# Mixture-of-experts combine: rounds of nine tokens with one summed on TensorE, in place of rounds of ten on VectorE

## The chip, the cores and the metric

The kernel runs on one core of a Trainium2 chip. The metric is the device time of one execution in microseconds (us). The profile's span, from the first to the last instruction, is a little shorter than that time.

## The reference

```python
batch, seq, n_experts, expert_dim = 16, 1024, 8, 512

def reference(expert_outputs, combine_weights):
    weights = combine_weights[..., np.newaxis]
    return np.sum(expert_outputs * weights, axis=2).astype(np.float32)
```

There are 16 x 1024 = 16,384 tokens. Each has eight expert outputs of 512 fp32 numbers (16 KB) and eight weights. The output of a token is the weighted sum of its eight rows (2 KB). Every input number is used once, so 268 MB come in and 34 MB go out, with a multiply and an add for each input number.

## The kernel before

Tokens lie on 128 partitions, so each partition has 128 tokens. "A token" below means one token on each partition: 128 x 16 KB. The tile `ring` holds ten tokens (`R = 10`). A round loads them in three chunks of four, four and two; a group, one pass of VectorE's hardware loop, is two rounds. Twelve rounds take 120 tokens; a tail of eight follows.

```python
R = 10
G = 2 * R
M = 2 * G
T_P = T // P
GROUPS = T_P // G
LOOP = GROUPS * G
TAIL = T_P - LOOP
ROUNDS = LOOP // R
CHUNKS = [(0, 4), (4, 4), (8, 2)]
# ... (cut)
x_g = x[0:cut].rearrange("(n p b g) e d -> n b p g e d", p=P, b=2, g=G)
# ... (cut)
pe_e = [6, 6, 6, 6, 5, 5, 5, 4]
tail_stores = [(0, 4), (4, 2), (6, 1), (7, 1)]
```

In the loop VectorE does all the arithmetic. For a chunk it makes one product with the first expert's weight, over all the chunk's tokens, and then for each token seven fused multiply-adds, each over 512 numbers. `take` waits on a semaphore and takes the amount off it again.

```python
with nc.Fori(0, GROUPS, engines=OrderedEngineSet([vector.engine])):
    for h in range(2):
        take(w_set[h], 1)
        for c, (r, m) in enumerate(CHUNKS):
            take(loaded[c], 16)
            q = h * R + r
            i = vector.tensor_tensor(
                out=acc[:, q : q + m],
                in0=ring[:, r : r + m, 0],
                in1=w_c[:, q : q + m, 0:1].to_broadcast([P, m, D]),
                op=mult,
            )
            # ... (cut)
            for g in range(q, q + m, 2):
                for e in range(1, E):
                    for k in (g, g + 1):
                        i = fused(k, e, w_c[:, k, e : e + 1], acc[:, k])
                        # ... (cut: waits and counts)
    take(step, last["all"])
```

SyncE issues the loads. A chunk is loaded again as soon as VectorE has finished its tokens of the round before. Once the loop's loads are out, the eight tail tokens are loaded one by one as slots come free, then the last round and the tail are stored.

```python
def loads_and_last_stores(sync):
    for n in range(ROUNDS):
        for c, (r, m) in enumerate(CHUNKS):
            if n:
                sync.wait_ge(done, (n - 1) * R + r + m)
            # ... (cut: the load of chunk c of round n; the weights after the first)
    for j in range(TAIL):
        sync.wait_ge(done, LOOP - R + j + 1)
        sync.dma_start(out=ring[:, j], in_=x_t[:, j]).then_inc(tail_in[j], 16)
    store(sync, ROUNDS - 1)
    for j, m in tail_stores:
        sync.wait_ge(done, LOOP + j + m)
        sync.dma_start(out=o_t[:, j : j + m], in_=acc[:, j : j + m]).then_inc(tail_out, 16)
```

ScalarE copies each round's weights to `w_c`, issues the stores of the other rounds, and in the tail multiplies the identity matrix by single weights, which gives diagonal matrices. TensorE multiplies them with the first four to six experts' rows of the tail tokens and sums in PSUM; VectorE does the other experts of the tail.

```python
def first_terms(tensor):
    for k, (j, e) in enumerate(diags):
        if e == 0:
            tensor.wait_ge(tail_in[j], 16)
        tensor.wait_ge(diag_set, k + 1)
        tensor.matmul(ps[:, j], lhsT=diag[:, k % DIAGS], rhs=ring[:, j, e],
                      start=e == 0, stop=e == pe_e[j] - 1).then_inc(product, 1)
```

Of the kernel before, what the change touches and what calls it, by code (L numbers as in the profile page):

```python
# [10 lines left out]
def kernel(  # L11
# [17 lines left out]

    nc = tc.nc  # L30
    fp32 = mybir.dt.float32
    mult, add = mybir.AluOpType.mult, mybir.AluOpType.add

    B, S, E, D = expert_outputs.shape
    T = B * S
    P = 128
    R = 10
    G = 2 * R
    M = 2 * G
    T_P = T // P  # L40
    GROUPS = T_P // G
    LOOP = GROUPS * G
    TAIL = T_P - LOOP
    ROUNDS = LOOP // R
    CHUNKS = [(0, 4), (4, 4), (8, 2)]
    C = len(CHUNKS)
    DIAGS = 5
# [3 lines left out]
    o = out.rearrange("b s d -> (b s) d")  # L51
    cut = LOOP * P
    x_g = x[0:cut].rearrange("(n p b g) e d -> n b p g e d", p=P, b=2, g=G)
    w_g = w[0:cut].rearrange("(n p m) e -> p n m e", p=P, m=M)
    o_g = o[0:cut].rearrange("(n p b g) d -> n b p g d", p=P, b=2, g=G)
    x_t = x[cut:T].rearrange("(p j) e d -> p j e d", j=TAIL)
    w_x = w[cut:T].rearrange("(p j) e -> p j e", j=TAIL)
    o_t = o[cut:T].rearrange("(p j) d -> p j d", j=TAIL)


    pe_e = [6, 6, 6, 6, 5, 5, 5, 4]
    tail_stores = [(0, 4), (4, 2), (6, 1), (7, 1)]
    diags = [(j, e) for j in range(TAIL) for e in range(pe_e[j])]
# [4 lines left out]
    acc = one.tile([P, G, D], fp32, name="acc")  # L68
    w_t = one.tile([P, T_P, E], fp32, name="w_t")
    w_c = one.tile([P, G, E], fp32, name="w_c")  # L70
    ident = one.tile([P, P], fp32, name="ident")
    diag = one.tile([P, DIAGS, P], fp32, name="diag")
    ps = psum.tile([P, TAIL, D], fp32, name="ps")
# [4 lines left out]
    loaded = [sem(f"loaded{c}") for c in range(C)]  # L78
    stored = [sem(f"stored{h}") for h in range(2)]
    step = sem("step")  # L80
    done = sem("done")
    tail_in = [sem(f"tail_in{j}") for j in range(TAIL)]
    tail_out = sem("tail_out")
    id_set = sem("id_set")
    diag_set = sem("diag_set")
    product = sem("product")

    def store(queue, n):
        h = n % 2
        queue.wait_ge(done, (n + 1) * R)  # L90
        queue.dma_start(
            out=o_g[n // 4, n // 2 % 2, :, h * R : h * R + R], in_=acc[:, h * R : h * R + R]
        ).then_inc(stored[h], 16)

    def loads_and_last_stores(sync):
        for n in range(ROUNDS):
            for c, (r, m) in enumerate(CHUNKS):
                if n:
                    sync.wait_ge(done, (n - 1) * R + r + m)
                g = n % 2 * R + r  # L100
                sync.dma_start(
                    out=ring[:, r : r + m], in_=x_g[n // 4, n // 2 % 2, :, g : g + m]
                ).then_inc(loaded[c], 16)
                if n == 0 and c == 0:
                    sync.dma_start(
                        out=w_t[:, 0:LOOP].rearrange("p (n m) e -> p n m e", m=M), in_=w_g
                    ).then_inc(w_in, 16)
                    sync.dma_start(out=w_t[:, LOOP:T_P], in_=w_x).then_inc(w_in, 16)
        for j in range(TAIL):
            sync.wait_ge(done, LOOP - R + j + 1)  # L110
            sync.dma_start(out=ring[:, j], in_=x_t[:, j]).then_inc(tail_in[j], 16)
        store(sync, ROUNDS - 1)
        for j, m in tail_stores:
            sync.wait_ge(done, LOOP + j + m)
            sync.dma_start(out=o_t[:, j : j + m], in_=acc[:, j : j + m]).then_inc(tail_out, 16)
# [13 lines left out]
    def weights_and_stores(scalar):  # L129
        scalar.wait_ge(w_in, 32)  # L130
        for n in range(ROUNDS):
            h = n % 2
            if n >= 2:
                store(scalar, n - 2)
                scalar.wait_ge(stored[h], 16 * (n // 2))
            scalar.copy(  # L136
                out=w_c[:, h * R : h * R + R], in_=w_t[:, n * R : n * R + R]
            ).then_inc(w_set[h], 1)
        store(scalar, ROUNDS - 2)
        scalar.wait_ge(stored[0], 16 * ROUNDS // 2)  # L140
        scalar.wait_ge(id_set, 2)
        for k, (j, e) in enumerate(diags):
            i = scalar.mul(out=diag[:, k % DIAGS], in_=ident, mul=w_t[:, LOOP + j, e : e + 1])  # L143
            i.then_inc(diag_set, 1)
            if k >= DIAGS:
                i.wait_op(product, k - DIAGS + 1, "sem-ge")
        scalar.wait_ge(stored[1], 16 * ROUNDS // 2)
        scalar.wait_ge(tail_out, 16 * len(tail_stores))

    def first_terms(tensor):  # L150
        for k, (j, e) in enumerate(diags):
            if e == 0:
                tensor.wait_ge(tail_in[j], 16)
            tensor.wait_ge(diag_set, k + 1)
            tensor.matmul(  # L155
                ps[:, j],
                lhsT=diag[:, k % DIAGS],
                rhs=ring[:, j, e],
                start=e == 0,
                stop=e == pe_e[j] - 1,  # L160
            ).then_inc(product, 1)

    def terms(vector):
        def take(s, v):
            vector.wait_ge(s, v).then_inc(s, -v)  # L165

        last = {}

        def count(i, g, e):

            if e == E - 1:
                i.then_inc(done, 1)
            else:
                i.then_inc(step, 1)
                last["all"] = last.get("all", 0) + 1
                last[g] = last["all"]

        def fused(g, e, weight, before):
            return vector.scalar_tensor_tensor(  # L179
                out=acc[:, g], in0=ring[:, g % R, e], scalar=weight, in1=before, op0=mult, op1=add  # L180
            )

        with nc.Fori(0, GROUPS, engines=OrderedEngineSet([vector.engine])):
            for h in range(2):
                take(w_set[h], 1)
                for c, (r, m) in enumerate(CHUNKS):
                    take(loaded[c], 16)
                    q = h * R + r
                    i = vector.tensor_tensor(  # L189
                        out=acc[:, q : q + m],  # L190
                        in0=ring[:, r : r + m, 0],
                        in1=w_c[:, q : q + m, 0:1].to_broadcast([P, m, D]),
                        op=mult,
                    )
                    i.then_inc(step, 1)
                    last["all"] = last.get("all", 0) + 1
                    last.update((g, last["all"]) for g in range(q, q + m))
                    for g in range(q, q + m, 2):
                        for e in range(1, E):
                            for k in (g, g + 1):  # L200
                                i = fused(k, e, w_c[:, k, e : e + 1], acc[:, k])
                                i.wait_op(step, last[k], "sem-ge")
                                count(i, k, e)
            take(step, last["all"])

        last.clear()
        for q in ((0, 1), (2,), (3,), (4,), (5,), (6,)):
            for e in range(pe_e[q[0]], E):
                for j in q:
                    weight = w_t[:, LOOP + j, e : e + 1]  # L210
                    if e == pe_e[j]:
                        i = fused(j, e, weight, ps[:, j])
                        i.wait_op(product, sum(pe_e[: j + 1]), "sem-ge")
                    else:
                        i = fused(j, e, weight, acc[:, j])
                        i.wait_op(step, last[j], "sem-ge")
                    count(i, j, e)

        j = TAIL - 1
        for e in range(pe_e[j], E):  # L220
            weight = w_t[:, LOOP + j, e : e + 1]
            if e == pe_e[j]:
                i = vector.tensor_scalar_mul(out=acc[:, j], in0=ring[:, j, e], scalar1=weight)  # L223
                i.wait_op(tail_in[j], 16, "sem-ge")
            else:
                i = fused(j, e, weight, acc[:, j])
                i.wait_op(step, last[j], "sem-ge")
            count(i, j, -1)
        vector.wait_ge(step, last[j])  # L229
        i = vector.tensor_tensor(out=acc[:, j], in0=acc[:, j], in1=ps[:, j], op=add)  # L230
        i.wait_op(product, len(diags), "sem-ge")
        count(i, j, E - 1)

    with tc.tile_critical(no_gpsimd_drain=True):  # L234
        loads_and_last_stores(nc.sync)
        identity(nc.gpsimd)
        weights_and_stores(nc.scalar)
        first_terms(nc.tensor)
        terms(nc.vector)
# [30 lines left out]
```

## Time and profile before

| | us |
|---|---|
| time, median of three | 707.33 (707.19 to 707.56) |
| span of the profiled execution | 705.5 |
| VectorE busy | 642.8 |
| TensorE busy, all of it in the tail | 38.7 |
| ScalarE busy | 21.1 |
| transfers in the span | 302.5 MB |

The profile's first part gives each engine's busy time and its share of the span. A second part cuts the span in 40 slices, with one digit of busy tenths for each, for the engines and for the 16 DMA engines together. The groups of instructions are listed by line, engine and operation, with the output and input tiles, their shapes, the count, the busy time, the mean length of one, and the idle time of that engine just before them with what ended it. Records of one engine may overlap, so that a mean can be longer than the pace at which instructions follow each other. DVE is VectorE, ACT ScalarE, PE TensorE, SP SyncE; a name with q is the engine's queue of waits and DMA issues.

### The profile page before, as it was taken

The page shows a single profiled execution, that of the slowest core. Times are in us where ns is not written, and L with a number is a line of the kernel's source. Part 1 is how long each engine was busy: PE and PEld are TensorE (multiplying, and loading weights), DVE is VectorE, ACT ScalarE, POOL GpSimd, SP SyncE. Part 2 cuts the span into 40 slices and gives each one's busy share as a digit, 9 for nine tenths or more (in the row PEclk, how much of TensorE's full clock was granted, in tenths as well). Part 3 has the DMA queues.
Part 4 walks back from the last instruction along what each step waited for, and adds up shares of the span by engine and source line. Part 5 has one row for each costly group of instructions (what it writes and reads, how often), then busy time and mean ns, then how long its engine had stood idle before and what let it go on. Part 6 is the DMA issues. An engine that isn't in the chain of part 4 may idle for free. (4 is left out here: it accounts for less than half of the span.)

```text
span 705.5 us, 1328 instructions
## 1 busy us (share of the span) xinstructions
PE 38.7 (5%) x86; PEld 16.9 (2%) x86; DVE 642.8 (91%) x898; ACT 21.1 (3%) x56; POOL 0.7 (0%) x6
## 2 busy tenths in 40 slices
PE   0000000000000000000000000000000000000695
PEld 0000000000000000000000000000000000000242
DVE  0599999979999989989999998998998998998964
ACT  0000000000000000000000000000000000000241
POOL 0000000000000000000000000000000000000000
PEclk9999999999999999999999999999999999999999
DMA  9999999999999999999999999999999999999997
GB/s 412 390 472 420 394 435 446 450 412 461 403 444 446 445 404 429 435 428 475 430 401 447 416 432 434 472 394 468 416 441 421 420 440 463 431 426 407 430 428 334
DMA packets 9186, 302.53 MB, mean 429 GB/s; under 512 B 1120, under 2 KB 1504, under 8 KB 1888
## 3 DMA queue, kind: packets, MB, share of 16 engines
q1 hardware_dynamic: 7600, 273.68, 90.0%
q10 hardware_dynamic: 1584, 28.84, 9.5%
q14 instruction: 2, 0.02, 0.0%
HBM read 268.96 MB, written 33.55 MB: 429 GB/s over the span
## 5 line engine op out<-in xcount | busy, mean ns | idle before, releaser
L179 DVE SCALAR_TENSOR_TENSOR acc<-ring,w_c,acc 128x512 f32<-128x512 f32 x840 | 559.7, 745 | 1.3
L189 DVE TENSOR_TENSOR acc<-ring,w_c 128x2048 f32<-128x2048 f32 (+1 forms) x36 | 69.5, 1931 | 46.2 <-DVEq L165 46.2
L155 PE MATMUL ps<-ring,diag 128*128 128x512 f32 x86 | 38.7, 613 | 659.1 <-DMA ring<-in_expert_outputs_dram 659.1
L155 PEld LDWEIGHTS ps<-ring,diag 128*128 128x128 f32 x86 | 16.9, 198 | 680.1 <-DMA ring<-in_expert_outputs_dram 659.1
L136 ACT COPY w_c<-w_t 128x80 f32<-128x80 f32 x12 | 3.0, 258 | 587.5 <-DMA out_dram<-acc 565.3
L143 ACT ACTIVATE diag<-ident,w_t 128x128 f32<-128x128 f32 x43 | 16.8, 400 | 84.4 <-DMA out_dram<-acc 54.2
L179 DVE SCALAR_TENSOR_TENSOR acc<-ring,w_t,ps 128x512 f32<-128x512 f32 x7 | 5.1, 744 | 9.6 <-PE ps L155 9.6
L179 DVE SCALAR_TENSOR_TENSOR acc<-ring,w_t,acc 128x512 f32<-128x512 f32 x13 | 9.7, 751 | 0.4
L136 ACT ACT_TABLE_LOAD x1 | 1.3, 1283 | 0.9 <-SPq L234 0.9
L230 DVE TENSOR_TENSOR acc<-acc,ps 128x512 f32<-128x512 f32 x1 | 0.7, 689 | 0.1
L223 DVE TENSOR_SCALAR acc<-ring,w_t 128x512 f32<-128x512 f32 x1 | 0.5, 481 | 0.0
L119 POOL TENSOR_SCALAR_AFFINE_SELECT ident<-ident 128x128 f32<-128x128 f32 x1 | 0.3, 292 | 0.1
L118 POOL MEMSET ident<- 128x128 f32 x1 | 0.2, 204 | 0.5 <-SPq L234 0.5
L254 POOL MEMSET const-bfloat16-1.0<- 128x1 bf16 x1 | 0.1, 101 | 0.0
L254 POOL MEMSET const-uint8-127<- 128x1 uint8 x1 | 0.1, 101 | 0.0
L254 POOL MEMSET const-float32-0.0<- 128x1 f32 x1 | 0.1, 98 | 0.2 <-issue 0.2
L254 POOL MEMSET const-float32-1.0<- 128x1 f32 x1 | 0.1, 98 | 0.0
## 6 DMA issues: line engine op xcount, KB each, us to landing
ring<-in_expert_outputs_dram SPq DMA_DIRECT2D x12, 4096.0 KB, 34.0
out_dram<-acc ACTq DMA_DIRECT2D x11, 2560.0 KB, 26.7
ring<-in_expert_outputs_dram SPq DMA_DIRECT2D x8, 2048.0 KB, 28.6
out_dram<-acc SPq DMA_DIRECT2D x1, 2560.0 KB, 24.8
out_dram<-acc SPq DMA_DIRECT2D x1, 1024.0 KB, 17.7
out_dram<-acc SPq DMA_DIRECT2D x1, 512.0 KB, 9.0
out_dram<-acc SPq DMA_DIRECT2D x2, 256.0 KB, 4.7
w_t<-in_combine_weights_dram SPq DMA_DIRECT2D x1, 480.0 KB, 22.6
```

The lines of the kernel that those rows point to most:

```text
L118: gpsimd.memset(ident, 0.0).then_inc(id_set, 1)
L119: gpsimd.affine_select(out=ident, in_=ident, compare_op=mybir.AluOpType.not_equal, fill=1.0, base=0, pattern=[[-1, P]], channel_multiplier ...
L136: scalar.copy(out=w_c[:, h * R : h * R + R], in_=w_t[:, n * R : n * R + R]).then_inc(w_set[h], 1)
L143: i = scalar.mul(out=diag[:, k % DIAGS], in_=ident, mul=w_t[:, LOOP + j, e : e + 1])
L155: tensor.matmul(ps[:, j], lhsT=diag[:, k % DIAGS], rhs=ring[:, j, e], start=e == 0, stop=e == pe_e[j] - 1,).then_inc(product, 1)
L179: return vector.scalar_tensor_tensor(out=acc[:, g], in0=ring[:, g % R, e], scalar=weight, in1=before, op0=mult, op1=add)
L189: i = vector.tensor_tensor(out=acc[:, q : q + m], in0=ring[:, r : r + m, 0], in1=w_c[:, q : q + m, 0:1].to_broadcast([P, m, D]), op=mult,)
L223: i = vector.tensor_scalar_mul(out=acc[:, j], in0=ring[:, j, e], scalar1=weight)
L230: i = vector.tensor_tensor(out=acc[:, j], in0=acc[:, j], in1=ps[:, j], op=add)
L254: nc = _bacc.Bacc("TRN2", target_bir_lowering=False, num_devices=1)
```

## The change

The ring holds nine tokens instead of ten, in three chunks of three. Fourteen rounds take 126 tokens and leave a tail of two. Per round VectorE sums eight tokens; the ninth, the last of the third chunk, goes to TensorE: VectorE makes all its eight diagonal matrices with one product, TensorE runs eight products in a loop of its own, and ScalarE copies the sum from PSUM to `acc`. This is meant to take work from VectorE, to leave little for the tail, and to have the slots come free in equal chunks. VectorE's loop is placed at a chosen instruction slot (`head_slot`), so that it begins in the second block of instructions. 126 tokens a partition are laid out as two blocks, 54 and 72 consecutive tokens on each partition, instead of three of 40. The stores of the last two rounds are held back until the tail's loads have been issued, and the tail is stored in one piece. In the tail TensorE does the first four experts and VectorE the last four.

The core of the diff:

```diff
-    R = 10
+    R = 9
+    C = 3
     G = 2 * R
-    M = 2 * G
+    BLOCKS = (6 * R, 8 * R)
# ... (cut: sizes and layouts)
+    HELD = 2
+    K = 4
# ...
     def loads_and_last_stores(sync):
         for n in range(ROUNDS):
-            for c, (r, m) in enumerate(CHUNKS):
+            for c in range(CHUNKS):
                 if n:
-                    sync.wait_ge(done, (n - 1) * R + r + m)
+                    sync.wait_ge(summed[c], n * C)
# ...
+        sync.wait_ge(summed[0], ROUNDS * C)
         for j in range(TAIL):
-            sync.wait_ge(done, LOOP - R + j + 1)
             sync.dma_start(out=ring[:, j], in_=x_t[:, j]).then_inc(tail_in[j], 16)
-        store(sync, ROUNDS - 1)
-        for j, m in tail_stores:
-            sync.wait_ge(done, LOOP + j + m)
-            sync.dma_start(out=o_t[:, j : j + m], in_=acc[:, j : j + m]).then_inc(tail_out, 16)
+        for n in range(ROUNDS - HELD, ROUNDS):
+            store(sync, n)
+        sync.wait_ge(done, 1)
+        sync.dma_start(out=o_t, in_=acc_t).then_inc(tail_out, 16)
# ... (ScalarE: weights and the tail's diagonals ahead of its rounds, then)
+        for n in range(ROUNDS):
+            if 1 <= n < ROUNDS - 1:
+                scalar.wait_ge(stored[(n - 1) % 2], 16 * ((n - 1) // 2 + 1))
+                weights(n + 1)
+            i = scalar.copy(out=acc[:, n % 2 * R + R - 1], in_=ps)
+            i.wait_op(product, (n + 1) * E, "sem-ge").then_inc(summed[-1], 1)
+            if n < ROUNDS - HELD:
+                store(scalar, n)
# ... (TensorE)
+        with nc.Fori(0, ROUNDS, engines=this):
+            take(tensor, fed, 1)
+            products(ps, diag, R - 1, E)
+        tensor.wait_ge(diag_set, TAIL * K)
+        for j in range(TAIL):
+            tensor.wait_ge(tail_in[j], 16)
+            products(ps_t[:, j], diag_t[:, j], j, K)
# ... (VectorE)
-        with nc.Fori(0, GROUPS, engines=OrderedEngineSet([vector.engine])):
+        with nc.Fori(0, ROUNDS // 2, engines=this, head_slot={vector.engine: 128}):
             for h in range(2):
-                take(w_set[h], 1)
-                for c, (r, m) in enumerate(CHUNKS):
-                    take(loaded[c], 16)
# ...
+                for c in range(CHUNKS):
+                    take(vector, loaded[c], 16)
+                    s = c * C
+                    g = h * R + s
+                    m = C
+                    if c == CHUNKS - 1:
+                        m = C - 1
+                        vector.tensor_tensor(
+                            out=diag,
+                            in0=ident[:, None, :].to_broadcast([P, E, P]),
+                            in1=w_c[:, g + m, :, None].to_broadcast([P, E, P]),
+                            op=mult,
+                        ).then_inc(fed, 1)
# ... (the first product over m tokens, then)
+                    for e in range(1, E):
+                        for k in range(m):
+                            weight = w_c[:, g + k, e : e + 1]
+                            i = fused(acc[:, g + k], ring[:, s + k, e], weight, acc[:, g + k])
+                            i.wait_op(step, last[k], "sem-ge")
+                            count(i, k, e, summed[c])
# ... (VectorE's tail: the last four experts of both tokens, then)
+        vector.wait_ge(step, last["all"])
+        vector.tensor_tensor(out=acc_t, in0=acc_t, in1=ps_t, op=add).wait_op(
+            product, ROUNDS * E + K * TAIL, "sem-ge"
+        ).then_inc(done, 1)
```

## The prediction

> **What bounds the kernel now.** I read the page first, then the stages of the span, then the chain of waits and VectorE's own waits, then VectorE's instructions in order of time. The page:
>
> ```profile
> span 705.5 us, 1328 instructions
> PE 38.7 (5%) x86; PEld 16.9 (2%) x86; DVE 642.8 (91%) x898; ACT 21.1 (3%) x56; POOL 0.7 (0%) x6
> DMA  9999999999999999999999999999999999999997
> HBM read 268.96 MB, written 33.55 MB: 429 GB/s over the span
> ```
>
> VectorE is busy 91% of the span and looks like the bound, but the DMA row is full from the first slice to the last. Which of the two ends last in a round is seen in VectorE's timeline, at the second chunk of a round (duration in us after the start time, then in brackets the idle time before it and what released it; L165 is the wait on a semaphore inside `take`):
>
> ```profile
> 262.07 2.29 DVE L189 TENSOR_TENSOR acc<-ring,w_c 128x2048 f32<-128x2048 f32 x1 [2.06 <-DVEq L165]
> 316.49 2.29 DVE L189 TENSOR_TENSOR acc<-ring,w_c 128x2048 f32<-128x2048 f32 x1 [2.04 <-DVEq L165]
> 370.93 2.29 DVE L189 TENSOR_TENSOR acc<-ring,w_c 128x2048 f32<-128x2048 f32 x1 [2.06 <-DVEq L165]
> ```
>
> In every round VectorE waits 2.06 us for a load, and rounds follow each other every 54.43 us. One token for each of 128 partitions is 128 x 16 KB = 2.097 MB in and 0.262 MB out, so a round of ten is 23.59 MB; over 54.43 us that is **433.4 GB/s**. The loop is bound by transfers, with VectorE 2 us behind them. The list of VectorE's waits agrees: 46.2 us in all, 24.9 of them for the first chunk.
>
> The rows of costs that I use (by line and shape; busy us, mean ns of one):
>
> ```profile
> L179 DVE SCALAR_TENSOR_TENSOR acc<-ring,w_c,acc 128x512 f32<-128x512 f32 x840 | 559.7, 745 | 1.3
> L189 DVE TENSOR_TENSOR acc<-ring,w_c 128x2048 f32<-128x2048 f32 x24 | 54.9, 2287 | 46.2 <-DVEq L165 46.2
> L189 DVE TENSOR_TENSOR acc<-ring,w_c 128x1024 f32<-128x1024 f32 x12 | 14.6, 1218 | 0.0
> L223 DVE TENSOR_SCALAR acc<-ring,w_t 128x512 f32<-128x512 f32 x1 | 0.5, 481 | 0.0
> ```
>
> The mean of a multiply-add is 745 ns, but 840 of them are busy only 559.7 us: their records overlap, and the pace is 559.7 / 840 = **0.666 us**. A round costs VectorE 70 x 0.666 + 2 x 2.29 + 1.22 = 52.4 us, which with the 2.06 us of waiting gives the 54.43.
>
> The end, from the chain of waits (start, us):
>
> ```profile
> 659.09 35.33 PE ps L155 x78
> ...
> 699.63 0.69 DVE acc L230
> ```
>
> TensorE's products end the tail of eight tokens. Transfers do not stop meanwhile: between 660 and 700 us the DMA share is 0.95 to 1.06, and it falls to 0.51 only in 700 to 704. After the last VectorE instruction ends, at 700.32, the store of one token (0.26 MB) and the end of the program take 5.2 us.
>
> **What the Trainium skill says.** "DMA: Bandwidth & Descriptors", section Bandwidth, puts the ceiling of one core's 16 ports at 435.2 GB/s. The 433.4 of a steady round is 0.4% below it, so the trace agrees, and a kernel that moves the same bytes can gain at most about 3 us in the loop. The same page, section Latency and other measured facts, says that copies slow down when the rows of the partitions lie a large power of two apart. Here the pitch is 40 tokens x 16 KB = 640 KB, no power of two, and the rate is full; the new pitches, 54 x 16 = 864 KB and 72 x 16 = 1152 KB, are none either. "Runtime: NRT & Kernel Launch", section Instruction fetch mechanics, says that a taken branch to a block of instructions no longer held stalls the engine for its fetch. The trace shows no such stall: at 129.48 us a new group of 20 tokens starts, straight after the multiply-adds that began at 120.20 and took 9.36. So placing the loop by hand can cure nothing visible here.
>
> **The change, part by part.**
>
> *Bytes.* Every input is still read once and every output written once, 302.5 MB. A round of nine takes 0.9 x 54.43 = 49.0 us of transfers at the present rate. Fourteen rounds plus two tokens replace twelve rounds plus eight. Loads become 48 KB a partition instead of 64 and 32, stores 18 KB instead of 20: packets of about the same size and number. Gain or loss: about 0.
>
> *VectorE.* A round needs 8 x 7 = 56 multiply-adds, 37.3 us; two first products of three tokens, for which I go between 1.22 us (1024 elements) and 2.29 (2048): 1.75 each; one of two tokens, 1.22; and one product that builds eight diagonals, 1024 elements of the same kind of instruction, 1.22. Sum **43.2 us**, 5.8 us under the transfers' 49.0, where before it was 2.0 under. All of this lies beside transfers that set the pace.
>
> *TensorE and ScalarE.* 43 products in the tail now take 38.7 us (two records for each), some 0.9 us each. Eight of them per round are about 7 us. From landing: 1.2 for the diagonals, 7 for the products, perhaps 0.6 for ScalarE's copy, some 9 us, against VectorE's 11.8 us for the same chunk (1.22 + 1.22 + 14 x 0.666). It is hidden.
>
> *The ring.* A slot's chunk is free 1.75 + 21 x 0.666 = 15.7 us after it lands if VectorE is waiting for it. Two other chunks, 29 us of loads without any store, are on their way then. The DMA queue doesn't run dry.
>
> *The start.* The chunk (2,1) landed at 153.9 us. Before it 28 tokens (58.7 MB), 5.1 MB of stores and 0.5 MB of weights had to move: 64.3 MB, at 433.4 GB/s 148.4 us. So the start costs **5.5 us** over the steady rate, latency of landing included. The first chunk is smaller now, but transfers, not VectorE, set the pace, so I leave the 5.5.
>
> *The end.* This is where the kernels differ. Let L be the landing of the last of the two tail tokens. Ahead of it goes all but the stores of the last two rounds (4.72 MB, held back) and the tail's output (0.52 MB): 297.3 MB, 686.0 us, so L = 686.0 + 5.5 = 691.5. The first chunk of the last round lands eight tokens earlier (16.8 MB, 38.7 us); from there VectorE is the slower one, 43.2 us for the round, and ends it at L + 4.5. Only then can the last round's store of 2.36 MB go out; the store of the round before, also 5.4 us, fills the time from L. Tail on VectorE: 2 x 0.48 + 6 x 0.666 = 5.0 and a sum of two tokens, about 1.3: L + 10.8. TensorE's eight products of the tail run beside it. Then the last store and the end, 5.2 us as before and 0.6 more for 0.26 MB more: L + 16.6 = **708.1 us** of span. The span before is 705.5. What is lost: stores held back leave transfers half idle while VectorE finishes a whole round and then the tail, where before single tokens kept being loaded and stored. Measured time lies 1.8 us over the span (707.33 against 705.5), so 709.9.
>
> **The rivals.**
>
> First, *VectorE's larger slack raises the transfer rate*. For it: VectorE is only 2 us behind now, and an occasional late release could cost an engine a gap. At 435.2 GB/s the whole would be 2.9 us shorter, and a cheaper start could give 1 or 2 more: 705 to 707. Against it: the period of 54.43 repeats to 0.02 us, and the queue is never seen empty. I give this a third, and shade the number by a little over 1 us.
>
> Second, *the new strides or sizes lower the rate*: 0.5% less would be 3.5 us more, 712 to 713. Nothing in this trace speaks for it, but nothing tests it.
>
> Third, *the sum on TensorE becomes a new wait*: if product and copy ended after VectorE's tokens, the third chunk would come free late. It would have to be over 10 us later before the loads starved. Unlikely; if each round lost 3 us, 750.
>
> Fourth, *VectorE was the true bound*, and 9 us less work per round shows. The 2.06 us waits speak against it; it would give well under 690.
>
> **Range and chances.** Sum 709.9, less the shade: **708.6 us**, 0.2% over before. The rate carries about 2.5 us each way, the end about 2, the start 1.5, together some 3.5: 704.5 to 712.5. Faster by over 2% would break the ceiling of the transfers; slower by over 2% needs a new wait in every round: 0.01, 0.97, 0.02.
>
> **What would show it.** Right: VectorE waits 5 to 6 us per round in the loop, its busy time between the same points is about 43 us, the period is 49.0 us, the DMA row stays full, and DMA thins out only in the last 10 us, with 10 to 11 us between the last tail landing and VectorE's last instruction. Wrong: a period other than 49.0 by over 0.2 (the rate, first or second rival), VectorE waiting on ScalarE's or TensorE's work (third), or a span between the last landing and the end well under 16 us, which would mean that I mis-sized the end.

## Result and profile after

The changed kernel takes 710.54 us (median of six runs, 709.66 to 710.66) against 707.26 for the kernel before: a ratio of **1.0042, 95% interval 1.0029 to 1.0055**. It is 3.3 us slower, clear of the noise and far inside 2%. The prediction was 708.6 with a range of 704.5 to 712.5; its unshaded sum was 709.9.

The page of the kernel after, the lines that answer to those shown of the kernel before:

```profile
span 708.6 us, 1616 instructions
PE 138.6 (20%) x240; PEld 56.7 (8%) x240; DVE 610.0 (86%) x849; ACT 15.2 (2%) x37; POOL 0.7 (0%) x6
DMA  8999999999999999999999999999999999999996
HBM read 268.96 MB, written 33.55 MB: 427 GB/s over the span
```

VectorE has lost 33 us of busy time and the span has grown by 3.1. The DMA row is full in both. VectorE's timeline in the middle of the loop (start, duration, then in brackets the idle time before and its releaser):

```profile
261.45 1.76 DVE L218 TENSOR_TENSOR acc<-ring,w_c 128x1536 f32<-128x1536 f32 x1 [2.25 <-DVEq L166]
280.75 1.76 DVE L218 TENSOR_TENSOR acc<-ring,w_c 128x1536 f32<-128x1536 f32 x1 [3.50 <-DVEq L166]
310.48 1.76 DVE L218 TENSOR_TENSOR acc<-ring,w_c 128x1536 f32<-128x1536 f32 x1 [2.27 <-DVEq L166]
```

A round takes 310.48 - 261.45 = 49.03 us for nine tokens, 21.23 MB, which is 433.1 GB/s; before, ten tokens took 54.43 us at 433.4. VectorE waits 2.25 + 3.50 us, some 5.8, in each round. So the work taken from VectorE became waiting.

The groups by line and shape (busy, mean ns of one, idle before):

```profile
L197 DVE SCALAR_TENSOR_TENSOR acc<-ring,w_c,acc 128x512 f32<-128x512 f32 x784 | 523.2, 746 | 1.5
L218 DVE TENSOR_TENSOR acc<-ring,w_c 128x1536 f32<-128x1536 f32 x28 | 49.2, 1757 | 90.5 <-DVEq L166 90.5
L212 DVE TENSOR_TENSOR diag<-ident,w_c 128x1024 f32<-128x1024 f32 x14 | 17.1, 1219 | 0.8 <-DVEq L166 0.8
L157 ACT COPY acc<-ps 128x512 f32<-128x512 f32 x14 | 8.2, 585 | 368.7 <-PE ps L171 368.7
```

The end, first from the chain of waits, then from VectorE's timeline:

```profile
686.39 10.18 PE ps L171 x16
696.57 6.88 PE ps_t L171 x16
703.45 0.02 issue
703.47 1.22 DVE acc_t L246
```

```profile
653.61 1.76 DVE L218 TENSOR_TENSOR acc<-ring,w_c 128x1536 f32<-128x1536 f32 x1 [2.26 <-DVEq L166]
...
687.41 9.37 DVE L197 SCALAR_TENSOR_TENSOR acc<-ring,w_c,acc 128x512 f32<-128x512 f32 x14
696.70 0.87 DVE L239 TENSOR_SCALAR acc_t<-ring,w_t 128x512 f32<-128x512 f32 x2
697.49 4.06 DVE L197 SCALAR_TENSOR_TENSOR acc_t<-ring,w_t,acc_t 128x512 f32<-128x512 f32 x6
```

From the landing of the last round's first chunk, 653.61, VectorE works without a pause until 701.55; then it waits 1.9 us for TensorE, whose last eight products queue behind those of the round. The eight of the round took 10.18 us, the eight of the tail 6.88. Meanwhile the transfers thin out (stretches of the span: the busy time and count of PE, of PEld, which is TensorE's loading of its left operand, of DVE, ACT and POOL; then the granted TensorE clock, the DMA share and GB/s):

```profile
692.00:696.00 4.00, 4.00 (x10) 1.59 (x9) 4.00 (x7) 0.00 (x0) 0.00 (x0) 0.93 0.76 327
696.00:700.00 4.00, 4.00 (x11) 1.85 (x10) 4.00 (x8) 0.59 (x1) 0.00 (x0) 1.00 0.54 226
700.00:704.00 4.00, 3.43 (x8) 1.17 (x7) 2.08 (x4) 0.00 (x0) 0.00 (x0) 1.00 0.87 369
704.00:708.00 4.00, 0.00 (x0) 0.00 (x0) 0.69 (x1) 0.00 (x0) 0.00 (x0) 0.78 0.32 131
```

In the kernel before, the transfers are still at full rate then:

```profile
692.00:696.00 4.00, 4.00 (x11) 1.75 (x10) 1.97 (x3) 1.07 (x3) 0.00 (x0) 1.00 1.02 439
696.00:700.00 4.00, 1.83 (x5) 0.53 (x3) 3.77 (x6) 0.00 (x0) 0.00 (x0) 1.00 0.95 401
```

### The profile page after: what moved, and what is told of

It reads as the page before. It is cut to its first block, busy times and chain, and to the rows that moved or that the text cites. A ratio compares the mean times of both kernels' runs of the same rounds, so it can differ in the third digit from the quotient of the medians.

```text
span 708.6 us, 1616 instructions
## 1 busy us (share of the span) xinstructions
PE 138.6 (20%) x240; PEld 56.7 (8%) x240; DVE 610.0 (86%) x849; ACT 15.2 (2%) x37; POOL 0.7 (0%) x6
## 5 line engine op out<-in xcount | busy, mean ns | idle before, releaser
L197 DVE SCALAR_TENSOR_TENSOR acc<-ring,w_c,acc 128x512 f32<-128x512 f32 x784 | 523.2, 746 | 1.5
L171 PE MATMUL ps<-ring,diag 128*128 128x512 f32 x224 | 131.8, 754 | 564.8 <-PEq L166 564.8
L218 DVE TENSOR_TENSOR acc<-ring,w_c 128x1536 f32<-128x1536 f32 (+1 forms) x42 | 66.3, 1578 | 90.5 <-DVEq L166 90.5
L171 PEld LDWEIGHTS ps<-ring,diag 128*128 128x128 f32 x224 | 53.7, 247 | 642.1 <-issue 642.1
L212 DVE TENSOR_TENSOR diag<-ident,w_c 128x1024 f32<-128x1024 f32 x14 | 17.1, 1219 | 0.8 <-DVEq L166 0.8
L157 ACT COPY acc<-ps 128x512 f32<-128x512 f32 x14 | 8.2, 585 | 368.7 <-PE ps L171 368.7
L140 ACT COPY w_c<-w_t 128x72 f32<-128x72 f32 x14 | 3.4, 251 | 292.6 <-DMA out_dram<-acc 292.6
L171 PE MATMUL ps_t<-ring,diag_t 128*128 128x512 f32 x16 | 7.0, 592 | 0.0
L197 DVE SCALAR_TENSOR_TENSOR acc_t<-ring,w_t,acc_t 128x512 f32<-128x512 f32 x6 | 4.1, 743 | 0.0
L171 PEld LDWEIGHTS ps_t<-ring,diag_t 128*128 128x128 f32 x16 | 3.0, 190 | 3.8 <-issue 3.8
```

The costliest lines, as they stand in the source:

```text
L140: scalar.copy(out=w_c[:, h * R : h * R + R], in_=w_t[:, n * R : n * R + R]).then_inc(w_set[h], 1)
L157: i = scalar.copy(out=acc[:, n % 2 * R + R - 1], in_=ps)
L171: tensor.matmul(out, lhsT=left_of[:, e], rhs=ring[:, j, e], start=e == 0, stop=e == terms - 1).then_inc(product, 1)
L197: return vector.scalar_tensor_tensor(out=out, in0=x, scalar=weight, in1=before, op0=mult, op1=add)
L212: vector.tensor_tensor(out=diag, in0=ident[:, None, :].to_broadcast([P, E, P]), in1=w_c[:, g + m, :, None].to_broadcast([P, E, P]), op=mul ...
L218: vector.tensor_tensor(out=acc[:, g : g + m], in0=ring[:, s : s + m, 0], in1=w_c[:, g : g + m, 0:1].to_broadcast([P, m, D]), op=mult,).the ...
```

## Experiments

Twelve runs follow, e10 of the unaltered changed kernel and e11 of e8's kernel again, each compared with the kernel before on the same chip (707.35 to 707.61 there). "The changed kernel" without a label is the run of the result, 710.54 us. Theory A: the loop is bound by transfers in both kernels, and the loss lies outside it, in the end.

### Is the loop bound by transfers?

**e1: TensorE's part taken back.** VectorE sums all nine tokens; diagonals, loop products and copy are gone.

```diff
-                    if c == CHUNKS - 1:
-                        m = C - 1
-                        vector.tensor_tensor(
-                            out=diag,
# ... (cut)
-                        ).then_inc(fed, 1)
# ... (cut: TensorE's loop, ScalarE's copy)
```

> VectorE sums all nine tokens of a round; TensorE and ScalarE do nothing in the loop. Theory A (the loop is bound by transfers, the loss lies in the end): VectorE's round grows to 63 x 0.666 + 3 x 1.76 = 47.2 us, still under 49.0, so the period stays at 49.0. In the end VectorE finishes the last round 4.3 us later than in the changed kernel, but no longer waits for TensorE, so its last instruction comes 2.5 us later: 713.0 us. Rival B (VectorE sets the pace of the loop): 14 x 4.1 = 57 us more. Rival C (the products and the copy in every round cost the loop something): under 710.5.

713.76 us, ratio 1.0089 (1.0075 to 1.0104). VectorE was busy 666.3 us instead of 610.0, and the time rose by only 3.2 us, all of it in the end: between 427.17 and 476.18 us a round still takes 49.0, and the last sum stands at 706.88 instead of 703.47. Rivals B and C are out.

**e2: VectorE lighter.** One expert is left out for the tokens that VectorE sums in the loop, so the output lacks these terms.

```diff
-                    for e in range(1, E):
+                    for e in range(2, E):
```

> The changed kernel leaves out one expert's multiply-add of each of VectorE's loop tokens (all loads and stores stay), 8 x 0.666 = 5.3 us less per round. Theory A: period 49.0 as before, gain only in the end; TensorE, whose eight products of the last round and eight of the tail follow the landing of the third chunk, then ends last, at about 701 instead of 703.5: 708 us. Rival B: 14 x 5.3 = 75 us less.

706.97 us, ratio 0.9994 (0.9986 to 1.0003): 3.6 us less than the changed kernel, not 75. Its chain of waits has the same form and ends earlier:

```profile
683.26 9.45 PE ps L171 x16
692.71 6.88 PE ps_t L171 x16
699.59 0.02 issue
699.61 1.22 DVE acc_t L246
```

VectorE reached the third chunk of the last round 3.1 us earlier, and with it TensorE's start moved from 686.39 to 683.26. In the loop 73 us of VectorE's work vanished, and the time does not show it.

**e3: one block of tokens.**

```diff
-    BLOCKS = (6 * R, 8 * R)
+    BLOCKS = (14 * R,)
```

> One block of 126 tokens on each partition instead of 54 and 72: other strides in HBM, one load of weights fewer. Theory A: the rate stays, 710.5 within 0.7. Rival D (the two-block layout costs rate): a difference of 2 us or more, and a period other than 49.0.

709.81 us, ratio 1.0033 (1.0023 to 1.0043), whose interval overlaps that of the changed kernel; it is 0.73 less, at the edge of the 0.7 expected. The last round's first chunk landed at 654.07 against 653.61, no earlier; what is shorter in the profile is TensorE's eight products of the last round, 8.95 us against 10.18. The layout of the tokens is not where the time went.

### Can the transfers go faster with two queues?

**e4: each load halved by partitions, one half on ScalarE's queue.**

```diff
+        q = slice(half * 64, half * 64 + 64)
+        queue.dma_start(
+            out=ring[q, c * C : c * C + C], in_=x_r[n][q, c * C : c * C + C]
+        ).then_inc(loaded[c], 16)
# ... (cut: SyncE calls it with half 0, ScalarE with half 1; VectorE waits for both)
```

> Every load of the loop is issued as two halves, partitions 0 to 63 on SyncE's queue and 64 to 127 on ScalarE's, so that both queues have loads under way at all times. Theory A: transfers are at their limit of 433 GB/s already, 710.5 within 1. Rival E (the rate is limited by one queue's gaps while no store runs beside the loads): period under 48.8 and 707 or less.

1295.57 us, ratio 1.8302 (1.8275 to 1.8328). Both expectations missed by far. The page of e4:

```profile
DMA  9999999999999999999999999999999999999996
DMA packets 9603, 302.55 MB, mean 235 GB/s; under 512 B 1792, under 2 KB 1920, under 8 KB 2176
```

The DMA row is as full as ever, at little over half the rate. A full row says only that packets are under way, not that they move at full speed: here the same row stands for 235 GB/s and, in the changed kernel, for 427.

**e5: the same, split by tokens,** two on SyncE's queue and one on ScalarE's, each over 128 partitions.

```diff
-        q = slice(half * 64, half * 64 + 64)
+        q = slice(c * C, c * C + 2) if half == 0 else slice(c * C + 2, c * C + C)
         queue.dma_start(
-            out=ring[q, c * C : c * C + C], in_=x_r[n][q, c * C : c * C + C]
+            out=ring[:, q], in_=x_r[n][:, q]
```

> As e4, but the halves are tokens, not partitions: of each chunk SyncE's queue loads two tokens and ScalarE's the third, each over all 128 partitions. Theory A ([...]the split by partitions made e4 slow; transfers over 128 partitions are at their limit with one queue): 710.5 within 2. Rival E (gaps of a single queue limit the rate): 707 or less, period under 48.8. Rival F (two queues with loads slow each other, whatever the shape): near 1290.

724.14 us, ratio 1.0225 (1.021 to 1.024). The third chunks of this kernel landed like this:

```profile
556.85 1.22 DVE L226 TENSOR_TENSOR diag<-ident,w_c 128x1024 f32<-128x1024 f32 x1 [3.13 <-DVEq L180]
...
655.32 1.23 DVE L226 TENSOR_TENSOR diag<-ident,w_c 128x1024 f32<-128x1024 f32 x1 [3.15 <-DVEq L180]
```

Two rounds in 98.47 us are 49.24 each, close to the 49.0 of one queue and no better: rivals E and F both fall. The 710.5 of theory A was missed too. So it was the 64-partition shape, with two queues alike, that halved the rate in e4. Why that shape is slow was not tried further. The extra time of e5 comes mostly at its start: three chunks share the transfers, and VectorE begins at 32.39 instead of 22.43. The rest was not taken apart.

### What in the end?

**e6: no store held back.**

```diff
-    HELD = 2
+    HELD = 0
```

> The changed kernel with no store held back: ScalarE issues the stores of the last two rounds like the others. Theory A: the store of the last round but one now runs beside the loads of the last round and delays its second and third chunks by up to 5 us, where VectorE has 1 to 2 us to spare; VectorE's last round ends 2 to 4 us later, 713 us. Rival G (holding back is what leaves transfers idle in the end): 708 or less.

713.76 us, ratio 1.0093 (1.0077 to 1.0108), 3.2 more than the changed kernel. VectorE now waits in the last round where it did not:

```profile
673.36 1.76 DVE L218 TENSOR_TENSOR acc<-ring,w_c 128x1536 f32<-128x1536 f32 x1 [3.50 <-DVEq L166]
```

Holding the stores back helps; rival G is out. I had listed the held stores as part of the loss; they are a remedy within this layout.

**e7: TensorE's token in the first chunk.** The copy moves ahead of the weights, and a store waits for both ends of the round.

```diff
-                    if c == CHUNKS - 1:
+                    if c == 0:
                         m = C - 1
# ... (cut)
```

> TensorE sums the first token of a round, in the first chunk, instead of the last token in the third. Work of every engine is the same. Theory A: in the loop nothing changes (period 49.0). In the end TensorE is free long before the tail lands, so VectorE's last sum no longer waits 1.9 us for it: 708.6. Rival H (TensorE's lateness is not what ends last; VectorE's own chain is): 710.5.

711.51 us, ratio 1.006 (1.0047 to 1.0074): slower by 1.0, where 1.9 less was expected; the intervals of the two overlap, so that only the missing gain is sure. The wait for TensorE is gone, as intended, and it gained nothing. VectorE's timeline shows why:

```profile
668.21 1.76 DVE L221 TENSOR_TENSOR acc<-ring,w_c 128x1536 f32<-128x1536 f32 x1 [1.61 <-DVEq L167]
...
683.92 1.75 DVE L221 TENSOR_TENSOR acc<-ring,w_c 128x1536 f32<-128x1536 f32 x1
...
704.59 1.22 DVE L249 TENSOR_TENSOR acc_t<-acc_t,ps_t 128x1024 f32<-128x1024 f32 x1
```

The second chunk landed at 668.2, and after it stand two full chunks of 15.7 us; in the changed kernel the second of them takes only 11.7. My expectation treated equal work per round as an equal end. What counts is the work behind the last landings, and here the token that TensorE takes over is worth more in the last chunk than in the first.

**e12: the kernel before with a coarse end.**

```diff
-    tail_stores = [(0, 4), (4, 2), (6, 1), (7, 1)]
+    tail_stores = [(0, 8)]
```

> The kernel before, with the eight tail tokens stored in one piece at the end instead of 4 + 2 + 1 + 1. Theory A (the kernel before keeps the transfers full to the end because finished tokens are stored while others are still summed): seven tokens, 1.84 MB, move after VectorE's last instruction instead of beside it, 1.84 / 0.433 = 4.2 us more, 711.5. Rival J (only VectorE's and TensorE's chain counts in the end, not the size of the stores): 707.3 and at most 1 more.

710.54 us, ratio 1.0041 (1.0027 to 1.0055): 3.2 more than before, a little under the 4.2 of the estimate. Its transfers idle while the tail is summed and then move the output (stretches as above):

```profile
695.00:700.00 5.00, 2.15 (x6) 0.60 (x4) 4.38 (x7) 0.00 (x0) 0.00 (x0) 1.00 0.34 147
700.00:705.00 5.00, 0.00 (x0) 0.00 (x0) 0.00 (x0) 0.00 (x0) 0.00 (x0) 0.74 0.99 419
```

The kernel before moves 411 GB/s from 695 to 700 us. Its fine-grained end is thus worth as much as the whole difference between the two kernels; rival J is out.

### The placement of the loop

**e8: the changed kernel without the placement.**

```diff
-        with nc.Fori(0, ROUNDS // 2, engines=this, head_slot={vector.engine: 128}):
+        with nc.Fori(0, ROUNDS // 2, engines=this):
```

> The changed kernel without the placement of VectorE's loop. Theory A: no stall of instruction fetch lies on the path, 710.5 within 0.7. Rival I (the placement spares a fetch in each of the seven passes): VectorE idles some time at each turn of the loop; with 5.8 us of slack per round this still moves the time by under 1 us, but the gap would be seen in VectorE's timeline.

709.05 us, ratio 1.0024 (1.0014 to 1.0033). That is 1.5 less than the changed kernel, and more than the 0.7 expected, so both ran again on one chip:

> The changed kernel, unaltered, on the same chip as e11, to compare the placement of the loop within one job. If the 1.5 us of e8 are real, 710.5; if they were the chip, the same as e11.

> The kernel of e8 again. If the placement costs time at the start, 709.0 and the first multiplication of VectorE 0.6 us or more earlier than in e10; if not, no difference to e10.

e10: 710.33 us, ratio 1.0034 (1.0023 to 1.0046). e11: 708.88 us, ratio 1.0023 (1.0015 to 1.0032). The difference of 1.45 us came again, though single runs of the two overlap (709.04 to 711.45 and 708.50 to 710.14), and so do the intervals. The last round's first chunk in e10, then in e11:

```profile
654.31 1.76 DVE L218 TENSOR_TENSOR acc<-ring,w_c 128x1536 f32<-128x1536 f32 x1 [2.26 <-DVEq L166]
```

```profile
652.79 1.76 DVE L218 TENSOR_TENSOR acc<-ring,w_c 128x1536 f32<-128x1536 f32 x1 [2.25 <-DVEq L166]
```

Nearly all of the 1.5 us is there already at 115.12 against 113.73 us, and 0.6 of it at VectorE's first instruction (22.41 against 21.78). VectorE is not late by itself: the weights, which ScalarE has to copy for it first, landed 0.6 us later, again e10 before e11:

```profile
20.61 1.28 ACT L140 ACT_TABLE_LOAD   x1 [20.61 <-DMA w_t<-in_combine_weights_dram]
```

```profile
19.98 1.28 ACT L140 ACT_TABLE_LOAD   x1 [19.98 <-DMA w_t<-in_combine_weights_dram]
```

In the first pair of profiles only 0.6 us is there by then (114.41 in the changed kernel, 113.83 in e8). No gap of VectorE at the turn of the loop appears without the placement; one that is shorter than the 2.25 us wait for a load there would stay unseen and cost nothing. So the placement costs about 1.45 us, 0.6 to 1.4 of it in the first 115 us, and gives nothing back here. By what way it delays the transfers the profile does not show; this stays open.

### A version that beats both

**e9: two tokens of a round on TensorE.** One in the second and one in the third chunk, with a second set of diagonals and a second PSUM bank; no placement; the tail's tokens are added up and stored one by one.

```diff
-                    if c == CHUNKS - 1:
+                    if c:
# ...
+            for d in range(2):
+                take(tensor, fed, 1)
+                products(ps[:, d], diag[:, d], C * (d + 2) - 1, E)
# ...
+        for j in range(TAIL):
+            sync.wait_ge(done, j + 1)
+            sync.dma_start(out=o_t[:, j], in_=acc_t[:, j]).then_inc(tail_out, 16)
```

> An attempt at a version that beats both: without the placement of the loop; TensorE sums the last token of the second and of the third chunk, so VectorE's round falls from 43.2 to about 39 us; the tail's two tokens are summed up and stored one by one. Theory A: period 49.0 still; the end gains what e2 gained (3.5 us), about 0.6 from the start as in e8, and about 1 from the smaller last sum and store: 705.5. Rival K (each added sum on TensorE and ScalarE costs the loop something): 710 or more.

**706.43 us, ratio 0.9985 (0.9978 to 0.9992)**: faster than the kernel before by 1.0 us, than the changed kernel by 3.9 (710.33, e10 on the same chip). It stayed 0.9 short of the 705.5 expected. The period stays at 49.0 (505.51 to 554.50 between first chunks), so rival K falls. The end of its VectorE timeline:

```profile
693.31 0.88 DVE L243 TENSOR_SCALAR acc_t<-ring,w_t 128x512 f32<-128x512 f32 x2
694.10 4.06 DVE L201 SCALAR_TENSOR_TENSOR acc_t<-ring,w_t,acc_t 128x512 f32<-128x512 f32 x6
698.27 1.29 DVE L251 TENSOR_TENSOR acc_t<-acc_t,ps_t 128x512 f32<-128x512 f32 x2
```

VectorE ends at 699.56, without waiting for TensorE, and from 695 to 700 us the transfers run at 424 GB/s, where the changed kernel had 192. The three parts of e9 were not run one by one.

## Why the prediction was right, point by point

- *The bound.* Right. The period is 49.03 us against 49.0, the wait 5.8 us as worked out, and e1 and e2 change VectorE's busy time by +56 and -73 us for +3.2 and -3.6.
- *VectorE's round.* 1.757 us for three tokens (1.75 estimated), 1.219 for the diagonals (1.22), a round of 43.1 (653.61 to 696.70, estimated 43.2).
- *The start.* The 5.5 us were kept from the kernel before, and L, the landing of the last tail token, was put at 691.5. The later of the two loads was issued at 669.8 and took 22.5: 692.3. Without the placement it landed at 691.6 (e8, issued at 669.1) and 691.5 (e11, at 669.0). So the missing 0.8 goes with the placement. "Placing the loop by hand can cure nothing visible here" held; that it could cost 1.45 us was not considered.
- *The end on VectorE.* Right: the last round ends at 696.7, L + 4.4 (L + 4.5 predicted), and VectorE's own part of the tail at L + 9.2 (L + 9.5).
- *TensorE in the end.* The term that failed. "TensorE's eight products of the tail run beside it" left out that they queue behind the eight of the last round, which begin only when VectorE, late by then, reaches the third chunk (686.39). Those eight were put at 7 us, from the tail of the kernel before, where TensorE works without a pause. After a pause of 36 us they took 10.18; in the mean of the fourteen rounds it was 131.8 / 14 = 9.4. The tail's eight, without a pause, took 6.88. At 7 and 7 TensorE would have been done at 700.4, before VectorE's 701.55, so it is the size that failed. "TensorE: Matmul & The Clock Gate", Part 1 (The HAM clock gate), says that an idle array falls to half the clock and needs some 3.4 us of work to come back. The trace agrees on the half: the granted clock is 0.50 from 656 to 692 us and 1.00 from 696 to 704. The way back took longer here: the products began at 686.39, and the clock still stood at 0.50 at 692. VectorE's last sum ended at L + 12.4 instead of L + 10.8. This size varies: in e10, the same kernel, the eight took 9.43 us, and VectorE waited 1.2 instead of 1.9:

```profile
703.43 1.22 DVE L246 TENSOR_TENSOR acc_t<-acc_t,ps_t 128x1024 f32<-128x1024 f32 x1 [1.18 <-PE ps_t L171]
```

- *TensorE in the loop.* "It is hidden" held, but barely. In the last round but one ScalarE's copy ended at 650.59 and VectorE's own tokens at 651.35: 0.8 us to spare, where 9 us against 11.8 was estimated.
- *The last store.* Too long: 5.8 us predicted, 3.9 measured from VectorE's end to the span's. In the kernel before the last two stores, of 256 KB each, took 4.7 us from issue to landing (median), with others ahead of them; in the changed one 512 KB took 2.6, since the store before it had landed. This error of 1.9 and TensorE's 1.6 nearly cancel, and 0.8 of the start is left over, so the close total of 708.1 against 708.6 owes something to luck.
- *What was lost.* The reasoning gave 2.6 us of span to the end. The runs divide the 3.1 otherwise: without the placement (e8, e11) the kernel is only 1.5 to 1.7 us over before, and the placement gives the other 1.45. What makes up the 1.5 to 1.7 is in part argued: e12 shows what a coarse end costs the kernel before, e9 gains with a finer end among two other changes, but no run gives the changed kernel a finer end alone. And the transfers thin out from 692 us on, 16 us before the end, where the prediction said the last 10.
- *The shade of 1.3 us* for a faster rate was unfounded: VectorE's wait nearly tripled, from 2.06 to 5.8 us a round, and the rate stayed at 433 GB/s.

## What to carry to other kernels

When every round waits for transfers, read a change's worth in the start and the end alone, and there count the work behind the last landings, not the work per round. Keep that work small and store finished pieces while others are still summed; take work off the busy engine in the last chunk first (e2, e7, e9 and e12 show it for this one). A sum that comes out right can hide two errors that cancel, so compare the terms and not only the total.

## What the runs showed of the hardware

With loads over 64 partitions, issued in pairs on two queues, the transfers ran at a mean of 235 GB/s with all DMA engines shown as busy (e4); the same two queues with 128-partition loads kept the rate of one queue within 0.5%. "DMA: Bandwidth & Descriptors", section Rules for kernel authors, says of two transfers to disjoint halves only that they serialize on the same engines and aren't worth the bother; here they cost a factor of 1.8, and no run shows by what way. And a hand-placed loop on an engine that is not the bound made the kernel 1.45 us slower (e10 against e11).
